# RMSNorm with SiLU on one core: loads and stores in strict turn on the GpSimd queue, 28 tiles ahead

## The chip, the cores and the metric

The kernel runs on one core of a Trainium2 chip. The core has a matrix engine (PE, not used here), VectorE (DVE), ScalarE (ACT), GpSimd (POOL) and SyncE (SP), each with its own instruction stream in program order, and 16 DMA engines that move data between the chip's memory (HBM) and the on-chip memory (SBUF, 128 partitions). Engines wait for each other and for DMAs through semaphores. The metric is device time in microseconds (us) of one execution, smaller being better; the median of several runs is compared.

## What is computed

The input `x` has 8 x 1024 rows of 2048 float32 values. Each row is divided by its root mean square, multiplied by `gamma`, and passed through SiLU:

```python
batch, seq_len, hidden = 8, 1024, 2048
...
rms = np.sqrt(np.mean(x ** 2, axis=-1, keepdims=True) + eps)
out = gamma * x / rms
return (out * (1 / (1 + np.exp(-out)))).astype(np.float32)
```

Input and output are 67.1 MB each, so 134 MB have to pass between HBM and the core.

## The kernel before

The 8192 rows are cut into 64 tiles of 128 rows; a row lies in one partition. In SBUF everything is bfloat16, while HBM holds float32, so each DMA converts: a load reads 8 KB a row and writes 4 KB, a store reads 4 KB and writes 8 KB. All DMAs are issued from GpSimd, on one queue, which the DMA engines work off in order.

`gamma` is first loaded into all partitions (tile `g`, L34). Then one loop over the 64 tiles does, for each of them:

- L42, GpSimd: load rows of `x` into `xt`
- L45, VectorE: `xg = xt * g`
- L48, VectorE: `xt * xt`, written over `xt`, with its row sums in `ss`
- L55, ScalarE: `rms = sqrt(ss / 2048 + eps)`
- L59, VectorE: `rstd = 1 / rms`
- L62, ScalarE: `ot = silu(rstd * xg)`
- L65, GpSimd: store `ot`

Sqrt and Silu use different tables of ScalarE, and where one follows the other the program has an `ACT_TABLE_LOAD`.

Each of `xt`, `xg` and `ot` has a pool of 8 buffers (`bufs=8`), so a load waits until the tile eight earlier has been read. The loop is written tile by tile, but the order that an engine gets is set by a scheduler, which moves instructions of neighbouring tiles past each other: on GpSimd, bursts of loads alternate with runs of stores, and Sqrt and Silu come in small batches. Every DMA on GpSimd counts up one of eight completion semaphores, taken in turn, and the ninth DMA waits for the first.

Of the kernel before, what the change touches and what calls it, by code (L numbers as in the profile page):

```python
# [1 line left out]

# [4 lines left out]


@with_exitstack  # L10
def kernel(
    ctx: ExitStack,
    tc: tile.TileContext,
    x: bass.AP,
    gamma: bass.AP,
    eps: bass.AP,
    out: bass.AP,
):
    nc = tc.nc
    P = nc.NUM_PARTITIONS  # L20
    bf16 = mybir.dt.bfloat16
    f32 = mybir.dt.float32
    x2 = x.flatten_outer_dims()
    o2 = out.flatten_outer_dims()
    n, d = x2.shape
    ntiles = (n + P - 1) // P

    singles = ctx.enter_context(tc.tile_pool(name="singles", bufs=1))
    pool = ctx.enter_context(tc.tile_pool(name="pool", bufs=8))
    small = ctx.enter_context(tc.tile_pool(name="small", bufs=8))  # L30

    g = singles.tile([P, d], bf16)
    gbc = bass.AP(tensor=gamma.tensor, offset=gamma.offset, ap=[[0, P], gamma.ap[0]])
    nc.gpsimd.dma_start(out=g, in_=gbc)  # L34
    eps_t = singles.tile([P, 1], f32)
    nc.vector.memset(eps_t, float(eps))  # L36

    for i in range(ntiles):
        s, e = i * P, min((i + 1) * P, n)
        ts = e - s  # L40
        xt = pool.tile([P, d], bf16)
        nc.gpsimd.dma_start(out=xt[:ts], in_=x2[s:e])  # L42

        xg = pool.tile([P, d], bf16)
        nc.vector.tensor_mul(out=xg[:ts], in0=xt[:ts], in1=g[:ts])  # L45

        ss = small.tile([P, 1], f32)
        nc.vector.tensor_tensor_reduce(  # L48
            out=xt[:ts], in0=xt[:ts], in1=xt[:ts],
            scale=1.0, scalar=0.0,  # L50
            op0=mybir.AluOpType.mult, op1=mybir.AluOpType.add,
            accum_out=ss[:ts],
        )
        rms = small.tile([P, 1], f32)
        nc.scalar.activation(out=rms[:ts], in_=ss[:ts],  # L55
                             func=mybir.ActivationFunctionType.Sqrt,
                             scale=1.0 / d, bias=eps_t[:ts])
        rstd = small.tile([P, 1], f32)
        nc.vector.reciprocal(out=rstd[:ts], in_=rms[:ts])  # L59

        ot = pool.tile([P, d], bf16)
        nc.scalar.activation(out=ot[:ts], in_=xg[:ts],  # L62
                             func=mybir.ActivationFunctionType.Silu,
                             scale=rstd[:ts])
        nc.gpsimd.dma_start(out=o2[s:e], in_=ot[:ts])  # L65


# [1 line left out]
_INS = ['x', 'gamma', 'eps']  # L69
_OUTS = [((8, 1024, 2048), 'float32')]  # L70
#: Inputs that are plain numbers.
_NUMBERS = {'eps': 9.999999747378752e-06}


# [26 lines left out]
```

## Time and profile before

| what | value |
|---|---|
| runs | 337.41, 339.43 and 339.48 us |
| median of the runs | 339.43 us |
| span of the profiled execution, first to last instruction | 336.1 us |
| busy: VectorE, ScalarE, GpSimd | 221.2, 219.1, 69.0 us |
| idle time of GpSimd before stores (L65), waiting for ScalarE | 221.4 us in 64 waits |
| idle time of VectorE before L45, waiting for loads | 95.7 us in 14 waits |
| idle time of ScalarE before L55 | 101.8 us |
| from issue to landing, median: load, store | 15.5 us, 11.5 us |

The profiled execution is listed by its span; the time outside of it is not listed, and the timed runs lie 1.3 to 3.4 us above the span. In a view of instruction groups, a row has the line, engine and operation, output <- input with shapes, the count, then busy time and mean duration (ns), then the idle time of the engine just before these instructions and what ended it. In the 40 slices, each digit is a busy share in tenths, and the row GB/s is what the DMAs wrote. A DMA share can exceed 1, since packets of one engine overlap a little.

### The profile page before, as it was taken

How to read it: one execution, taken by the hardware profiler on the slowest of the kernel's cores; microseconds unless marked ns; L12 is line 12 of the kernel's file. 1: busy time of each engine (PE TensorE's matmuls, PEld its weight loads, DVE VectorE, ACT ScalarE, POOL GpSimd, SP SyncE). 2: the span in 40 equal slices, each digit the busy share in tenths (PEclk: the TensorE clock that was granted, in tenths of full speed). 3: DMA queues.
4: the chain of work that ended last, by engine and by line, in shares of the span. 5: the costliest groups of instructions: out<-in, count | busy, mean ns of one | idle time of the engine just before them, and what ended most of it. 6: DMA issues, size and time to landing. Idle time of an engine off the chain costs nothing.

```text
span 336.1 us, 838 instructions
## 1 busy us (share of the span) xinstructions
DVE 221.2 (66%) x257; ACT 219.1 (65%) x188; POOL 69.0 (21%) x133
## 2 busy tenths in 40 slices
DVE  0999990407999914099999030899991308999900
ACT  1486977522869795238697761386978613869792
POOL 6012111050111110501111105011111050111110
DMA  7999999899999998999999989999999799999997
GB/s 140 212 214 254 335 398 363 332 312 208 214 288 327 402 365 321 324 214 214 291 316 414 366 325 310 214 212 319 307 424 367 286 297 214 213 311 309 420 429 273
DMA packets 18582, 101.24 MB, mean 301 GB/s; under 512 B 2064, under 2 KB 2064, under 8 KB 10384
## 3 DMA queue, kind: packets, MB, share of 16 engines
q0 software_dynamic: 18576, 101.20, 104.1%
q14 instruction: 6, 0.05, 0.0%
HBM read 68.16 MB, written 67.11 MB: 402 GB/s over the span
## 4 chain that ended last, share of the span: by engine, by line
issue 72%; POOL 14%; DMA 11%; POOLq 1%; PEldq 0%
DMA xt<-in_x_dram 11%; POOL out_dram L65 10%; POOL xt L42 4%; POOLq L65 0%; POOL g L34 0%; POOLq L96 0%; POOLq L42 0%; PEldq L96 0%
## 5 line engine op out<-in xcount | busy, mean ns | idle before, releaser
L48 DVE CUSTOM_DVE_ANT_0 xt<-xt 128x2048 bf16<-128x2048 bf16 x64 | 144.8, 2280 | 0.3
L45 DVE TENSOR_TENSOR xg<-xt,g 128x2048 bf16<-128x2048 bf16 x64 | 76.6, 1217 | 95.7 <-DMA xt<-in_x_dram 95.7
L62 ACT ACTIVATE ot<-xg,rstd 128x2048 bf16<-128x2048 bf16 x64 | 124.4, 1993 | 5.8 <-DVE rstd L59 5.5
L55 ACT ACTIVATE rms<-ss,eps_t 128x1 f32<-128x1 f32 x64 | 17.8, 292 | 101.8 <-DVE ss L48 63.7
L65 POOL DMA_DIRECT2D out_dram<-ot x64 | 34.2, 534 | 221.4 <-ACT ot L62 221.4
L42 POOL DMA_DIRECT2D xt<-in_x_dram x64 | 34.1, 554 | 38.8 <-DVE ss L48 22.8
L55 ACT ACT_TABLE_LOAD x30 | 38.5, 1283 | 2.1 <-DVE ss L48 1.0
L62 ACT ACT_TABLE_LOAD x30 | 38.5, 1283 | 0.5
L59 DVE RECIPROCAL rstd<-rms 128x1 f32<-128x1 f32 x64 | 8.6, 153 | 8.4 <-ACT rms L55 8.4
L48 DVE DVE_READ_ACCUMULATOR2_ANT ss<- 128x1 f32 x64 | 5.2, 81 | 0.0
L34 POOL DMA_DIRECT2D g<-in_gamma_dram x1 | 0.7, 667 | 0.8 <-PEq L96 0.8
L36 DVE MEMSET eps_t<- 128x1 f32 x1 | 0.1, 59 | 0.8 <-PEq L82 0.8
L82 POOL MEMSET const-float32-0.0<- 128x1 f32 x1 | 0.1, 99 | 0.2 <-issue 0.2
L82 POOL MEMSET const-bfloat16-1.0<- 128x1 bf16 x1 | 0.1, 102 | 0.0
L82 POOL MEMSET const-float32-1.0<- 128x1 f32 x1 | 0.1, 99 | 0.0
L82 POOL MEMSET const-uint8-127<- 128x1 uint8 x1 | 0.1, 99 | 0.0
## 6 DMA issues: line engine op xcount, KB each, us to landing
out_dram<-ot POOLq DMA_DIRECT2D x64, 1024.0 KB, 11.5
xt<-in_x_dram POOLq DMA_DIRECT2D x64, 512.0 KB, 15.5
g<-in_gamma_dram POOLq DMA_DIRECT2D x1, 512.0 KB, 4.7
```

Of the source, the lines that this page charges most:

```text
L34: nc.gpsimd.dma_start(out=g, in_=gbc)
L36: nc.vector.memset(eps_t, float(eps))
L42: nc.gpsimd.dma_start(out=xt[:ts], in_=x2[s:e])
L45: nc.vector.tensor_mul(out=xg[:ts], in0=xt[:ts], in1=g[:ts])
L48: nc.vector.tensor_tensor_reduce(out=xt[:ts], in0=xt[:ts], in1=xt[:ts], scale=1.0, scalar=0.0, op0=mybir.AluOpType.mult, op1=mybir.AluOpTy ...
L55: nc.scalar.activation(out=rms[:ts], in_=ss[:ts], func=mybir.ActivationFunctionType.Sqrt, scale=1.0 / d, bias=eps_t[:ts])
L59: nc.vector.reciprocal(out=rstd[:ts], in_=rms[:ts])
L62: nc.scalar.activation(out=ot[:ts], in_=xg[:ts], func=mybir.ActivationFunctionType.Silu, scale=rstd[:ts])
L65: nc.gpsimd.dma_start(out=o2[s:e], in_=ot[:ts])
L82: nc = _bacc.Bacc("TRN2", target_bir_lowering=False, num_devices=1)
```

## The change

The whole loop is written anew; four things differ.

- **Order of DMAs.** 28 loads are issued ahead of everything (`LEAD`), and from then on each store is followed by the load of the tile 28 further on, as long as there is one.
- **Buffers.** There is one tile name, `xt`, with 40 buffers. The product with `g` and the Silu are written in place, and the squares go to two scratch tiles that nobody reads (`sq` for ScalarE, `junk` for VectorE).
- **Statistics by fours.** Four tiles share one `ss`, one Sqrt and one reciprocal on 128x4.
- **Squares on two engines.** The sum of squares of even tiles moves to ScalarE (`Square` with an accumulator, L73), that of odd tiles stays on VectorE (L75).

`GRAIN` is 1, so `rows` and `lanes` give whole tiles.

```diff
+    BUFS, LEAD, GRAIN = 40, 28, 1
...
-    pool = ctx.enter_context(tc.tile_pool(name="pool", bufs=8))
+    pool = ctx.enter_context(tc.tile_pool(name="pool", bufs=BUFS))
...
+    def load(i, j):
+        if j == 0:
+            xts[i] = pool.tile([P, d], bf16, name="xt")
+        nc.gpsimd.dma_start(out=lanes(xts[i], j), in_=rows(x2, i, j))
...
+    for i in range(LEAD):
+        for j in range(GRAIN):
+            load(i, j)
...
+        if k % 2 == 0:
+            nc.scalar.activation(out=sq, in_=xts[i], func=ACT.Square, accum_out=acc)
+        else:
+            nc.vector.tensor_tensor_reduce(out=junk, in0=xts[i], in1=xts[i], scale=1.0, scalar=0.0,
+                                           op0=ALU.mult, op1=ALU.add, accum_out=acc)
...
+        nc.scalar.activation(out=rms, in_=ss, func=ACT.Sqrt, scale=1.0 / d, bias=eps_t)
...
+        for i in range(b * GROUP, (b + 1) * GROUP):
+            nc.vector.tensor_mul(out=xts[i], in0=xts[i], in1=g)
+        for i in range(b * GROUP, (b + 1) * GROUP):
+            k = i % GROUP
+            xt = xts.pop(i)
+            nc.scalar.activation(out=xt, in_=xt, func=ACT.Silu, scale=rstd[:, k:k + 1])
+            for j in range(GRAIN):
+                nc.gpsimd.dma_start(out=rows(o2, i, j), in_=lanes(xt, j))
+                if i + LEAD < ntiles:
+                    load(i + LEAD, j)
+
+    for b in range(ntiles // GROUP):
+        for i in range(b * GROUP, (b + 1) * GROUP):
+            stats(i)
+        norm(b)
```

What this does to GpSimd's queue is seen best in its instruction list. `DMASW0` to `DMASW7` are the eight completion semaphores of its DMAs; `DVE` and `Activation` are waits for VectorE and ScalarE. Before, from the eighth load on (the seven before it wait for nothing):

```order
L42 DMA xt<-in_x_dram 128x2048 [waits DMASW0_49]
L42 DMA xt<-in_x_dram 128x2048 [waits DMASW1_49,DVE_49]
L65 DMA out_dram<-ot 128x2048 [waits DMASW2_49,Activation_49]
L42 DMA xt<-in_x_dram 128x2048 [waits DMASW3_49,DVE_49]
L65 DMA out_dram<-ot 128x2048 [waits DMASW4_49,Activation_49]
L65 DMA out_dram<-ot 128x2048 [waits DMASW5_49,Activation_49]
L42 DMA xt<-in_x_dram 128x2048 [waits DMASW6_49,DVE_49]
L42 DMA xt<-in_x_dram 128x2048 [waits DMASW7_49,DVE_49]
L65 DMA out_dram<-ot 128x2048 [waits DMASW0_49,Activation_49]
L65 DMA out_dram<-ot 128x2048 [waits DMASW1_49,Activation_49]
```

After, on the same engine, where the 28 loads end and the pairs begin:

```order
L51 DMA xt<-in_x_dram 128x2048 [waits DMASW2_49]
L51 DMA xt<-in_x_dram 128x2048 [waits DMASW3_49]
L51 DMA xt<-in_x_dram 128x2048 [waits DMASW4_49]
L93 DMA out_dram<-xt 128x2048 [waits DMASW5_49,Activation_49]
L51 DMA xt<-in_x_dram 128x2048 [waits DMASW6_49]
L93 DMA out_dram<-xt 128x2048 [waits DMASW7_49,Activation_49]
L51 DMA xt<-in_x_dram 128x2048 [waits DMASW0_49]
```

The first store now stands behind 28 loads, where it stood behind nine, loads wait for DMAs alone and no longer for VectorE, and loads and stores take strict turns.

On ScalarE, before, a stretch early in the program:

```order
L55 ACT_TABLE_LOAD
L55 ACTIVATE rms<-ss,eps_t 128x1 x3
L62 ACT_TABLE_LOAD
L62 ACTIVATE ot<-xg,rstd 128x2048 x3
L55 ACT_TABLE_LOAD
```

After, its beginning, from the first Square on (`sq` is the scratch tile for squares):

```order
L73 ACTIVATE sq,ss<-xt 128x2048 x3
L83 ACT_TABLE_LOAD
L83 ACTIVATE rms<-ss,eps_t 128x4
L73 ACTIVATE sq,ss<-xt 128x2048
L91 ACT_TABLE_LOAD
L91 ACTIVATE xt<-xt,rstd 128x2048 x4
```

Squares of the following group now stand ahead of a group's Silus, so the first Silu waits for tile 6 as well; a group of four has one Sqrt on 128x4 and two table loads.

More of the change, by code (lines that the diff above doesn't have):

```diff
@@ L7 @@
 from concourse._compat import with_exitstack
+ACT = mybir.ActivationFunctionType
+ALU = mybir.AluOpType
 @with_exitstack
@@ L25, with rows, lanes @@
     n, d = x2.shape
-    ntiles = (n + P - 1) // P
+    ntiles = n // P
+    BUFS, LEAD, GRAIN = 40, 28, 1
     singles = ctx.enter_context(tc.tile_pool(name="singles", bufs=1))
-    pool = ctx.enter_context(tc.tile_pool(name="pool", bufs=8))
+    pool = ctx.enter_context(tc.tile_pool(name="pool", bufs=BUFS))
     small = ctx.enter_context(tc.tile_pool(name="small", bufs=8))
+    def rows(t, i, j):
+        return t[i * P:(i + 1) * P].rearrange("(p g) d -> g p d", g=GRAIN)[j]
+    def lanes(t, j):
+        if GRAIN == 1:
+            return t
+        return t[j:P:GRAIN]
+    xts = {}
+    def load(i, j):
+        if j == 0:
+            xts[i] = pool.tile([P, d], bf16, name="xt")
+        nc.gpsimd.dma_start(out=lanes(xts[i], j), in_=rows(x2, i, j))
     g = singles.tile([P, d], bf16)
@@ L36 @@
     nc.vector.memset(eps_t, float(eps))
[L38 to L65, printed above, removed]
+    sq = singles.tile([P, d], bf16)
@@ new lines, with stats @@
+    for i in range(LEAD):
+        for j in range(GRAIN):
+            load(i, j)
+    GROUP = 4
+    var = {}
+    def stats(i):
+        k = i % GROUP
+        if k == 0:
+            var[i // GROUP] = small.tile([P, GROUP], f32, name="ss")
+        acc = var[i // GROUP][:, k:k + 1]
+        if k % 2 == 0:
[3 more added lines that the diff above has]
+                                           op0=ALU.mult, op1=ALU.add, accum_out=acc)
@@ new lines, with norm @@
+    junk = singles.tile([P, d], bf16, name="junk")
+    def norm(b):
+        ss = var.pop(b)
+        rms = small.tile([P, GROUP], f32, name="rms")
+        nc.scalar.activation(out=rms, in_=ss, func=ACT.Sqrt, scale=1.0 / d, bias=eps_t)
+        rstd = small.tile([P, GROUP], f32, name="rstd")
+        nc.vector.reciprocal(out=rstd, in_=rms)
+        for i in range(b * GROUP, (b + 1) * GROUP):
+            nc.vector.tensor_mul(out=xts[i], in0=xts[i], in1=g)
+        for i in range(b * GROUP, (b + 1) * GROUP):
+            k = i % GROUP
+            xt = xts.pop(i)
[4 more added lines that the diff above has]
+                    load(i + LEAD, j)
```

## The prediction

> **What bounds the kernel now.** I read the page's list of engines first, then its 40 slices.
>
> ```profile
> DVE 221.2 (66%) x257; ACT 219.1 (65%) x188; POOL 69.0 (21%) x133
> ...
> DVE  0999990407999914099999030899991308999900
> ACT  1486977522869795238697761386978613869792
> ...
> DMA  7999999899999998999999989999999799999997
> GB/s 140 212 214 254 335 398 363 332 312 208 214 288 327 402 365 321 324 214 214 291 316 414 366 325 310 214 212 319 307 424 367 286 297 214 213 311 309 420 429 273
> DMA packets 18582, 101.24 MB, mean 301 GB/s; under 512 B 2064, under 2 KB 2064, under 8 KB 10384
> ```
>
> VectorE and ScalarE are each idle for a third of the span; the DMA row is not. Its GB/s counts the bytes written, so a load (1.049 MB of float32 read, 0.524 MB of bfloat16 written) counts half of what a store counts (1.049 MB written). The level near 213 and the level near 427 are therefore the same pace, which pure stretches show best. The next rows are those of a table of stretches: from:to, length, busy time (and instructions) of DVE, ACT and POOL, clock, DMA share, GB/s.
>
> ```profile
> core 0: us, DVE busy (x) ACT busy (x) POOL busy (x), PEclk, DMA share, GB/s
> 8.00:24.00 16.00, 15.06 (x17) 9.79 (x9) 2.13 (x4) 1.00 1.06 213
> ...
> 312.00:328.00 16.00, 7.62 (x12) 13.83 (x13) 2.35 (x5) 1.00 1.12 428
> ...
> 28.50:65.50 37.00, 25.33 (x33) 27.82 (x24) 4.80 (x9) 1.00 1.10 368
> ```
>
> Loads alone run at 213: 0.5243 MB / 213 GB/s = 2.46 us each. Stores alone run at 428: 1.0486 / 428 = 2.45 us each. The third row mixes them: it moves 13.6 MB, which is 4 loads and 11 stores (2.10 + 11.53 MB), 15 DMAs in 37.0 us or 2.47 us each. So a DMA of one tile costs the same 2.46 us in every company. The program has 129 of them (gamma, 64 loads, 64 stores): 34.08 MB / 213 GB/s = 160.0 us and 67.11 MB / 428 GB/s = 156.8 us, together 316.8 us of the 336.1. The kernel is bound by its DMAs, and what a rearrangement can win is the other 19.3 us. I looked for them with the same table:
>
> ```profile
> 0.00:3.00 3.00, 0.06 (x1) 1.28 (x1) 1.94 (x8) 1.00 0.11 20
> 25.00:28.50 3.50, 3.50 (x4) 1.73 (x3) 1.60 (x3) 1.00 1.06 157
> 65.00:68.00 3.00, 0.00 (x0) 3.00 (x2) 0.53 (x1) 1.00 0.30 112
> 74.00:77.00 3.00, 0.00 (x0) 0.00 (x0) 0.53 (x1) 1.00 0.99 146
> 132.00:135.00 3.00, 0.00 (x0) 3.00 (x2) 0.53 (x1) 1.00 0.21 79
> 199.00:202.00 3.00, 0.00 (x0) 2.98 (x3) 0.53 (x1) 1.00 0.40 150
> 207.00:210.00 3.00, 0.00 (x0) 0.00 (x0) 0.53 (x1) 1.00 1.05 178
> 265.00:269.00 4.00, 0.00 (x0) 3.98 (x3) 0.53 (x1) 1.00 0.33 125
> 275.00:278.00 3.00, 0.02 (x1) 0.00 (x0) 0.53 (x1) 1.00 0.95 147
> 330.00:331.00 1.00, 0.00 (x0) 0.00 (x0) 0.28 (x1) 1.00 0.91 344
> 333.00:336.10 3.10, 0.00 (x0) 0.00 (x0) 0.00 (x0) 1.00 0.14 50
> ```
>
> They are of three kinds.
> - Ends. The first 3 us do the work of 20/213 x 3 = 0.3 us, so 2.7 are lost; the last 3.1 do 50/428 x 3.1 = 0.36, so 2.7 are lost.
> - Dry queue. At 65, 132, 199 and 265 the DMA share falls to 0.2 to 0.4: nothing is queued. Lost against 428: 2.2, 2.4, 1.9 and 2.8 us, and 0.2 before the last store, 9.5 in all.
> - Slow but occupied. At 25, 74, 207 and 275 the share stays near 1 and the rate is low. Lost against 213: 0.9, 0.9, 0.5 and 0.9 us, 3.3 in all.
>
> 5.4 + 9.5 + 3.3 = 18.2 of the 19.3; about 1 us is spread thinly. The chain of waits says little here: 72% of it is "issue", GpSimd sitting between DMAs. The waits and the timeline of GpSimd say why the queue runs dry:
>
> ```profile
> POOL out_dram L65 <- ACT ot L62: 221.4, 64, 10.6
> DVE xg L45 <- DMA xt<-in_x_dram: 95.7, 14, 14.0
> ...
> POOL xt L42 <- DMA out_dram<-ot: 6.6, 4, 2.0
> ...
> 6.20 0.53 POOL L42 DMA_DIRECT2D xt<-in_x_dram  x1 [0.56 <-DMA g<-in_gamma_dram]
> ...
> 66.56 0.53 POOL L65 DMA_DIRECT2D out_dram<-ot  x1 [10.58 <-ACT ot L62]
> 68.45 0.53 POOL L65 DMA_DIRECT2D out_dram<-ot  x1 [1.36 <-ACT ot L62]
> 68.97 3.72 POOL L42 DMA_DIRECT2D xt<-in_x_dram  x7
> ```
>
> One in-order queue carries both directions. GpSimd stands 10.6 us at a store whose tile is not computed; the loads for the next tiles stand behind it and go out in a burst only at 68.97. Meanwhile the DMAs empty the queue. VectorE then waits for the burst (95.7 us in all), and the round repeats every 67 us. The line at 6.20 shows a second limit: the ninth DMA waited for the landing of the first (gamma), though it reads nothing of it. Eight completion semaphores serve the queue in turn, so eight DMAs can be outstanding.
>
> **The change part by part.**
>
> *Order on GpSimd.* Gamma and 28 loads go first, then 36 pairs of store and load, then 28 stores. The count of DMAs is unchanged, 129, and no other queue takes any, so 316.8 us of transfers stay. Each DMA still waits for the eighth before it to land. Behind that wait stand all later loads and stores, but seven more DMAs are in flight, 7 x 2.46 = 17 us of cover, against 4.7 us from issue to landing for gamma:
>
> ```profile
> g<-in_gamma_dram POOLq DMA_DIRECT2D x1, 512.0 KB, 4.7
> ```
>
> So this wait costs nothing. GpSimd's issuing, 129 x 0.54 = 70 us spread over the span, is hidden the same way.
>
> *Buffers.* Tile i+28 takes the buffer of tile i-12, whose store stands 24 DMAs earlier in the same queue; the semaphore wait eight back already implies it. No cost.
>
> *Is a store ready when its place comes?* ScalarE's first group runs three Squares, Sqrt, a fourth Square and then the Silus, so store 0 needs tile 6.
>
> ```profile
> 8.57 1.22 DVE L45 TENSOR_TENSOR xg<-xt,g 128x2048 bf16<-128x2048 bf16 x1 [7.70 <-DMA xt<-in_x_dram]
> ...
> L48 DVE CUSTOM_DVE_ANT_0 xt<-xt 128x2048 bf16<-128x2048 bf16 x64 | 144.8, 2280 | 0.3
> L45 DVE TENSOR_TENSOR xg<-xt,g 128x2048 bf16<-128x2048 bf16 x64 | 76.6, 1217 | 95.7 <-DMA xt<-in_x_dram 95.7
> L62 ACT ACTIVATE ot<-xg,rstd 128x2048 bf16<-128x2048 bf16 x64 | 124.4, 1993 | 5.8 <-DVE rstd L59 5.5
> L55 ACT ACTIVATE rms<-ss,eps_t 128x1 f32<-128x1 f32 x64 | 17.8, 292 | 101.8 <-DVE ss L48 63.7
> ...
> L55 ACT ACT_TABLE_LOAD x30 | 38.5, 1283 | 2.1 <-DVE ss L48 1.0
> ```
>
> Tile 0 has landed at 8.6, tile 6 at 8.6 + 6 x 2.46 = 23.3, and after a Square, a table load and a Silu the first output is there at about 29. Its place in the queue is the 30th: 3 + 29 x 2.46 = 74 us. That is 45 us of cover.
>
> *Work per group of four tiles.* A Square is not in the trace; it lies between the Sqrt of 128x1 (0.29 us) and twice the Silu of the same tile (4 us), and I take the Silu's 2.0, the same shape. ScalarE: 2 Squares 4.0, 2 table loads 2.6, one Sqrt 0.3, 4 Silus 8.0 = 14.9 us. VectorE: 2 x 2.28 + 4 x 1.22 and small ones = 9.8 us. The DMAs of four tiles take 8 x 2.46 = 19.7 us, so both stay hidden; with a Square at 4 us ScalarE is at 18.9 and just so. After the prefill ScalarE works off its backlog and then waits for loads, far ahead of the stores. At the end load 63 is the 101st DMA (3 + 101 x 2.46 = 251 us), its group is done some 20 us later, and store 60 moves only at 3 + 125 x 2.46 = 310. So statistics by fours and the in-place tiles cost nothing; if that cover were gone, a store would be late again as at 65 us.
>
> *Dry stretches*: 9.5 us go, all of them.
>
> *Changes of direction.* The mixed stretch held 15 DMAs that by the pure rates take 4 x 2.46 + 11 x 2.45 = 36.8 us, and took 37.0 with 7 changes: 0.03 us each. The new order has 72: 2.1 us, bounds 0 and 2.1.
>
> *Slow but occupied stretches.* Three of four follow a burst of eight loads behind stores, which is no longer there; the first, in the prefill, I keep: 0.9 us, bounds 0 and 3.3.
>
> *Sum.* 316.8 + 5.4 (ends) + 2.1 + 0.9 = 325.2 us of span, against 336.1. What lies outside the span isn't in the page; the timed runs were 337.4 to 339.5 (median 339.4), so 1.3 to 3.4 us above it. With the median's 3.3 I predict 328.5 us, 3.2% faster.
>
> **The rivals.**
>
> *The directions overlap.* If a DMA engine's reading and writing ran side by side, a load (8 KB read, 4 KB written a row) next to a store (4 KB read, 8 KB written) would need 12 KB of time for the pair and not 16: 36 pairs x 4.91 x 1/4 = 44 us less, 284 us. For it: loads write at half the rate at which stores write, so something is idle in each. Against it: the mixed stretch, with whole DMAs alternating as they will now, shows 2.47 us per DMA. The Trainium skill, DMA: Bandwidth & Descriptors, section "Terms", names the two halves of a transfer, reading side and writing side, from which one would hope for this. [...]
>
> *Each turn from store to load stalls.* The rows at 74, 207 and 275 each lie a little behind such a turn and lost 0.5 to 0.9 us, 0.8 on average. Place: the 36 pairs. At that price 36 x 0.8 = 29 us, on 328.5 less about 1 us for those turns counted above: 356 us, slower. Against it: the mixed stretch has three such turns and lost 0.2 us in all. It decides from (339.4 - 328.5) / 36 = 0.3 us a turn, ten times what the mixed stretch shows.
>
> *ScalarE becomes the bound.* If a Square took over 4.4 us (19.7 - 10.9 = 8.8 for two), a group would outlast its transfers. At 6 us: 16 x 22.9 + some 25 at the ends = 391 us. Only an unknown in the accumulating form speaks for it.
>
> **How the numbers follow.** Chances: the queue stays full, 0.84; overlap, 0.03; stalls at turns, 0.10 (half of it at 0.2 to 0.4 us a turn, which is no change); ScalarE the bound, 0.03. The first case alone: low 322.2 + 1.3 = 323.5, less 1 or 2 for the rounding of the rates; high 322.2 + 2.1 + 3.3 + 3.4 = 331. The range goes a little into the stalls, 321.5 to 334. About 1% is what a measurement of this kernel can tell from no change: faster by over 1% 0.87, within 1% 0.05, slower 0.08.
>
> **What would show it.** Right: in the slices the DMA row stays at 9 from the second to the last but one, the GB/s row has three levels (213 for some 70 us, about 318 for 177 us, 428 for 69 us), GpSimd waits mostly for DMA landings eight back and no longer for ScalarE, and ScalarE waits for loads. Wrong: a dip of DMA share inside the span, a middle level well off 318 (higher: overlap; lower: stalls), or stores waiting for Silu late in the program.

## The result, and the profile after

The changed kernel takes 324.67 us (median of four runs, 324.63 to 324.72), the kernel before 339.02 us in the runs beside it (337.41 to 339.48). The ratio is 0.9585, with an interval of 0.9562 to 0.9609: 4.2% faster. The forecast was 328.5 us, in a range of 321.5 to 334. The profiled execution has a span of 322.9 us and a time of 324.65 us.

The page of the changed kernel, its engines and its slices:

```profile
DVE 148.4 (46%) x145; ACT 232.2 (72%) x177; POOL 69.1 (21%) x133
...
DVE  0479897864838474352744543754337410000000
ACT  1449999999999999978949398599799993000000
...
DMA  7999999999999999999999999999999999999997
GB/s 128 214 215 212 213 216 212 212 216 313 308 344 305 318 341 300 326 334 297 334 325 301 339 314 309 343 305 318 343 296 328 400 425 432 426 424 433 425 428 270
DMA packets 18582, 101.24 MB, mean 314 GB/s; under 512 B 2064, under 2 KB 2064, under 8 KB 10384
```

The DMA row is 9 from the second slice to the last but one. The GB/s row has the three levels of the new order: loads alone at 213, pairs of store and load around 320, stores alone at 428. VectorE and ScalarE have nothing left to do in the last six slices, while the stores still queued are written out.

The table of stretches of the changed kernel (columns as before: from:to, length, busy time of DVE, ACT and POOL, clock, DMA share, GB/s), at the start, where two of the old holes were, in the phase of the pairs, and at the end:

```profile
0.00:3.00 3.00, 0.06 (x1) 1.28 (x1) 1.94 (x8) 1.00 0.26 22
3.00:6.00 3.00, 0.00 (x0) 0.00 (x0) 2.64 (x5) 1.00 0.96 184
...
65.00:68.00 3.00, 0.81 (x2) 2.96 (x5) 0.53 (x1) 1.00 1.05 210
74.00:77.00 3.00, 2.42 (x3) 3.00 (x3) 0.56 (x2) 1.00 1.12 386
...
80.00:240.00 160.00, 82.65 (x81) 138.10 (x105) 34.71 (x65) 1.00 1.09 321
...
320.00:322.90 2.90, 0.00 (x0) 0.00 (x0) 0.00 (x0) 1.00 0.04 11
```

A pair writes 1.049 + 0.524 = 1.573 MB. At 321 GB/s it takes 4.90 us, 2.45 us a DMA, the price of the pure stretches: turning the direction with every DMA costs nothing that can be measured.

The waits of the changed kernel, the longest totals first (engine, line, what it waited for: total us, times, longest):

```profile
POOL out_dram L93 <- DMA out_dram<-xt: 97.9, 47, 2.2
POOL xt L51 <- DMA xt<-in_x_dram: 96.4, 56, 2.0
DVE junk L75 <- DMA xt<-in_x_dram: 86.5, 22, 10.5
...
POOL out_dram L93 <- ACT xt L91: 17.8, 7, 4.5
```

GpSimd now waits for landings eight DMAs back, about 2 us at a time and with seven DMAs still queued. The last row still puts 17.8 us down to Silu, where it was 221.4 us before, but these too are waits for landings: a wait for several semaphores is put down to the one that moved last, and the tiles had long been done. The view of tile `xt` has the first and the last start of the Silus and of the stores (after the durations in ns):

```profile
L91 ACT ACTIVATE xt<-xt,rstd x64: 1984/1986/2003, 27.1 to 267.4; 128x2048 bf16<-128x2048 bf16 x64
L93 POOL DMA_DIRECT2D out_dram<-xt x64: 533/538/542, 58.6 to 302.1; - x64
```

Taken pair by pair in the trace, every Silu ended 29 to 74 us before GpSimd issued its store; for the store with the wait of 4.5 us it was 48 us. No store was late.

### The profile page after: what moved, and what is told of

The parts are those of the page before. It is cut to its first block, busy times and chain, and to the rows that moved or that the text cites. A ratio compares the mean times of both kernels' runs of the same rounds, so it can differ in the third digit from the quotient of the medians.

```text
span 322.9 us, 639 instructions
## 1 busy us (share of the span) xinstructions
DVE 148.4 (46%) x145; ACT 232.2 (72%) x177; POOL 69.1 (21%) x133
## 4 chain that ended last, share of the span: by engine, by line
DMA 88%; issue 3%; ACT 2%; POOL 1%; POOLq 0%; DVE 0%; PEldq 0%
DMA xt<-in_x_dram 70%; DMA out_dram<-xt 18%; ACT xt L91 2%; POOL xt L51 0%; POOL g L55 0%; POOLq L131 0%; DVE rstd L85 0%; DVE ss L75 0%; POOLq L93 0%; DVE junk L75 0%; PEldq L131 0%
## 5 line engine op out<-in xcount | busy, mean ns | idle before, releaser
L91 ACT ACTIVATE xt<-xt,rstd 128x2048 bf16<-128x2048 bf16 x64 | 122.9, 1990 | 21.3 <-DVE rstd L85 21.1
L75 DVE CUSTOM_DVE_ANT_0 junk<-xt 128x2048 bf16<-128x2048 bf16 x32 | 73.3, 2290 | 86.5 <-DMA xt<-in_x_dram 86.5
L87 DVE TENSOR_TENSOR xt<-xt,g 128x2048 bf16<-128x2048 bf16 x64 | 75.5, 1217 | 12.2 <-ACT sq L73 9.0
L73 ACT ACTIVATE sq<-xt 128x2048 bf16<-128x2048 bf16 x32 | 60.8, 1901 | 14.5 <-DMA xt<-in_x_dram 14.1
L93 POOL DMA_DIRECT2D out_dram<-xt x64 | 34.3, 536 | 135.0 <-DMA out_dram<-xt 97.9
L85 DVE RECIPROCAL rstd<-rms 128x4 f32<-128x4 f32 x16 | 2.8, 175 | 12.7 <-ACT rms L83 12.7
L73 ACT ACTIVATION_READ_ACCUMULATOR sq<-xt 128x1 f32 x32 | 6.0, 186 | 0.0
L83 ACT ACTIVATE rms<-ss,eps_t 128x4 f32<-128x4 f32 x16 | 4.8, 297 | 0.2
L75 DVE DVE_READ_ACCUMULATOR2_ANT ss<- 128x1 f32 x32 | 2.6, 83 | 0.0
```

The lines of the kernel that those rows point to most:

```text
L73: nc.scalar.activation(out=sq, in_=xts[i], func=ACT.Square, accum_out=acc)
L75: nc.vector.tensor_tensor_reduce(out=junk, in0=xts[i], in1=xts[i], scale=1.0, scalar=0.0, op0=ALU.mult, op1=ALU.add, accum_out=acc)
L83: nc.scalar.activation(out=rms, in_=ss, func=ACT.Sqrt, scale=1.0 / d, bias=eps_t)
L85: nc.vector.reciprocal(out=rstd, in_=rms)
L87: nc.vector.tensor_mul(out=xts[i], in0=xts[i], in1=g)
L91: nc.scalar.activation(out=xt, in_=xt, func=ACT.Silu, scale=rstd[:, k:k + 1])
```

## The experiments

Each was timed beside the kernel before, which had medians of 338.9, 338.8 and 338.2 us in the three groups (runs 1 to 4, 5 to 8, 9 to 12).

**1. The kernel before once more.** No edit.

> The kernel before, unchanged, to see what comes back at the same place. Theory: the four dry stretches (DMA share 0.2 to 0.4 near 65, 132, 199 and 265 us) are set by the order of the program and come back there, 9 to 10 us in all; the slow but occupied stretches are an effect of the moment and move or differ in size; the time lies 1.7 to 1.8 us above the span, as after the change. Rival: the slow stretches are made by the program too (by bursts of eight loads) and come back at 74, 207 and 275 us with 0.5 to 0.9 us each.

Measured: 339.06 us (337.5 to 340.04); the profiled execution took 338.78 us with a span of 337.0. The same table of it:

```profile
25.00:28.50 3.50, 3.50 (x4) 1.92 (x4) 1.60 (x3) 1.00 1.02 169
65.00:68.00 3.00, 0.00 (x0) 3.00 (x2) 0.53 (x1) 1.00 0.28 107
74.00:77.00 3.00, 0.08 (x1) 0.00 (x0) 0.53 (x1) 1.00 1.05 179
132.00:135.00 3.00, 0.00 (x0) 3.00 (x2) 0.53 (x1) 1.00 0.07 25
141.00:144.00 3.00, 0.00 (x0) 0.00 (x0) 0.53 (x1) 1.00 1.02 158
199.00:202.00 3.00, 0.00 (x0) 3.00 (x2) 0.53 (x1) 1.00 0.20 74
208.00:211.00 3.00, 0.00 (x0) 0.00 (x0) 0.53 (x1) 1.00 1.01 156
266.00:270.00 4.00, 0.00 (x0) 3.98 (x3) 0.53 (x1) 1.00 0.42 158
275.00:278.00 3.00, 0.00 (x0) 0.00 (x0) 0.53 (x1) 1.00 1.02 154
```

The dry stretches are back in place: 2.2, 2.8, 2.5 and 2.5 us against 428 GB/s, 10.0 us. The four slow but occupied stretches are back in place too, 0.5 to 0.8 us each, and there is a fifth at 141 us, 0.8 us, where the first profile had 206 GB/s and lost 0.1 us. So the rival was right on the places, which belong to this program; how much is lost at each differs between executions. The time outside the span is 1.8 us here and 1.75 us after the change.

**2. More buffers, same order.**

```diff
-    pool = ctx.enter_context(tc.tile_pool(name="pool", bufs=8))
+    pool = ctx.enter_context(tc.tile_pool(name="pool", bufs=14))
```

> The kernel before with 14 buffers for each of its three tiles; GpSimd's order stays exactly the same. Theory (the order makes the queue run dry, since a store that is not ready holds the loads behind it): the dry stretches stay, time 333 to 339 us. Rival (buffers were short): 325 to 328 us.

Measured: 339.01 us, ratio 1.0005 (0.9979 to 1.0031). GpSimd's instructions come in the same order as before, and the dry stretches stay: 175 GB/s from 66 to 69 us, 38 from 132 to 135, 55 from 267 to 270. Buffers alone do nothing as long as stores hold the loads behind them in the queue.

**3. The order alone.** The arithmetic of before, tile by tile, three tiles, all squares on VectorE; 24 loads ahead, then store and load in turn. The loads get 32 buffers, and the product and the output five each, where before had eight.

```diff
-    pool = ctx.enter_context(tc.tile_pool(name="pool", bufs=8))
+    xpool = ctx.enter_context(tc.tile_pool(name="xpool", bufs=32))
+    pool = ctx.enter_context(tc.tile_pool(name="pool", bufs=5))
+    LEAD = 24
...
+    for i in range(LEAD):
+        load(i)
...
+        if i + LEAD < ntiles:
+            load(i + LEAD)
```

> The arithmetic of before, tile by tile, with three tiles and all squares on VectorE, but 24 loads ahead and then stores and loads in turn. Theory (the order alone wins): 324.5 to 327 us, as long as ScalarE holds 4.9 us a tile; its 94 table loads, 64 Sqrts and 64 Silus come to 263 us, 4.1 us a tile. Rival (the grouping by fours is needed, since Sqrt, reciprocal and Silu of one tile wait for each other): ScalarE at 5.2 us a tile or more, stores late, 335 to 345 us.

Measured: 334.18 us, ratio 0.9866 (0.9843 to 0.9889): a third of the gain, outside the range of the theory and just short of the rival's. The queue was full for 288 us, and then ran dry four times, among the last stores:

```profile
288.00:292.00 4.00, 3.88 (x4) 4.00 (x3) 0.53 (x1) 1.00 0.43 162
301.00:304.00 3.00, 2.97 (x4) 3.00 (x3) 0.69 (x2) 1.00 0.40 150
310.00:314.00 4.00, 3.96 (x5) 3.99 (x3) 0.53 (x1) 1.00 0.27 100
320.00:323.00 3.00, 0.00 (x0) 3.00 (x2) 0.53 (x1) 1.00 0.35 131
```

Against 428 GB/s that is 2.5 + 1.9 + 3.1 + 2.1 = 9.6 us. ScalarE is busy throughout in these rows: once only stores are left, the queue takes a tile every 2.45 us, and ScalarE's lead was used up. Where the lead was lost stands in the waits of this kernel:

```profile
ACT ot L69 <- DMA out_dram<-ot: 29.1, 4, 23.0
```

The first store could move only behind 24 loads, the five output buffers were full long before, and ScalarE stood 23 us. In the phase of the pairs it could not win them back: with one tile at a time it has two table loads of 1.28 us, a Sqrt of 0.29 and a Silu of 2.00, together 4.85 us, and a pair takes 4.91.

**4. All squares on VectorE, in the changed kernel.**

```diff
-        if k % 2 == 0:
+        if False:
```

> The changed kernel with all squares on VectorE. VectorE then has 64 x 2.29 + 64 x 1.22 = 225 us and ScalarE 172 us. Theory (both lie beside the DMAs): the same 324.5 to 325.0 us. Rival (VectorE's 3.6 us a tile with its waits delays stores): over 326 us.

Measured: 324.83 us (324.75 to 324.91), with VectorE busy 218.6 us and ScalarE 168.7. Splitting the squares over two engines is worth 0.2 us at most.

**5 and 6. Shorter leads, in the changed kernel.**

```diff
-    BUFS, LEAD, GRAIN = 40, 28, 1
+    BUFS, LEAD, GRAIN = 20, 7, 1
```

> The changed kernel with LEAD 7 and 20 buffers; the scheduler puts 12 loads first and soon settles on store i, load i+7. A group's statistics then need a load that was issued only a few DMAs before the group's first store. Theory (a full queue is all that counts): the queue runs dry once a group, some 2 to 8 us in each of about 14 groups, 350 to 430 us. Rival (seven tiles ahead are enough): 325 us.

```diff
-    BUFS, LEAD, GRAIN = 40, 28, 1
+    BUFS, LEAD, GRAIN = 20, 12, 1
```

> The changed kernel with LEAD 12 and 20 buffers. Between the load of a group's last tile and the group's first store stand 16 DMAs, 39 us, and a group's work is some 15 us. Theory (a full queue is all that counts): 324.5 to 325.2 us, as with 28. Rival (the depth of 28 tiles is needed): 328 us or more.

Measured: 327.81 us with 7 tiles, 325.61 us with 12. The forecast for 7 was far off, and 12 lies 0.4 us above its range. With 7 tiles the scheduler put a group's squares behind the Silus of the group before, so no group waited for loads of the next. GpSimd still stood up to 12 us before a group's first store (222.0 us of waits for Silu in all), but eight queued DMAs are 8 x 2.46 = 19.7 us of work and bridged that. Before the last four stores no loads are left to queue; there GpSimd stood 14.1 us, and one dry stretch is left:

```profile
310.00:315.00 5.00, 0.00 (x0) 4.99 (x4) 1.06 (x2) 1.00 0.50 188
```

That is 5 x (1 - 188/428) = 2.8 us of the 3.1 us between this kernel and the changed one. With 12 tiles no dry stretch is left; 0.9 us remain, of which a slow but occupied stretch before the first store (33 to 36 us, 186 GB/s) is 0.4.

**7. Stores on another queue.** Silu writes float32 tiles, and SyncE stores them without converting; 16 loads ahead, 24 buffers, eight output tiles.

```diff
-            nc.scalar.activation(out=xt, in_=xt, func=ACT.Silu, scale=rstd[:, k:k + 1])
+            yt = ypool.tile([P, d], f32, name="yt")
+            nc.scalar.activation(out=yt, in_=xt, func=ACT.Silu, scale=rstd[:, k:k + 1])
             for j in range(GRAIN):
-                nc.gpsimd.dma_start(out=rows(o2, i, j), in_=lanes(xt, j))
+                nc.sync.dma_start(out=rows(o2, i, j), in_=lanes(yt, j))
```

> The changed kernel with Silu writing float32 tiles, which SyncE stores on its own queue without converting; loads stay on GpSimd, 16 ahead, 24 buffers. Loads and stores now alternate packet by packet inside a DMA engine. Theory (a DMA engine works on one packet at a time and 8 KB a row cost the same in any company): 129 x 2.455 = 316.7 us stay, 323 to 327 us. Rival (reading and writing overlap once they alternate finely): below 310 us.

Measured: 328.79 us, 1.8 us above the range of the theory. In the phase with both directions:

```profile
80.00:240.00 160.00, 75.93 (x75) 120.88 (x94) 17.08 (x33) 1.00 1.04 316
```

316 GB/s against 321 in the changed kernel, which over 160 us is about 2.5 of the 4.2 us by which the span is longer. Two queues that offer both directions at the same time move no more than one queue that turns with every tile, so reading and writing do not overlap to any gain here.

**8 and 12. Gamma as one row.** One row of 8 KB is loaded, and TensorE spreads it over the partitions; in run 12 its DMA goes third, behind two loads.

```diff
-    nc.gpsimd.dma_start(out=g, in_=gbc)
+    nc.gpsimd.dma_start(out=grow, in_=g1)
+    ones = singles.tile([1, P], bf16, name="ones")
+    nc.vector.memset(ones, 1.0)
...
+    for c in range(0, d, 512):
+        nc.tensor.matmul(gp[:, c:c + 512], lhsT=ones, rhs=grow[:, c:c + 512], start=True, stop=True)
+    nc.vector.tensor_copy(out=g, in_=gp)
```

> The changed kernel, with gamma loaded as one row of 8 KB and spread to the partitions by TensorE (four matmuls with a column of ones) and one copy, in place of a DMA of 128 rows. Theory (each whole DMA costs 2.46 us of the end): 322.1 to 322.5 us. Rival (the first DMA is hidden in the start-up): 324.7 us.

> The kernel with gamma as one row, its small DMA issued behind the first two loads and not ahead of them. Theory (the small DMA ahead of all others delayed the first load by 0.4 us): 322.4 to 322.7 us. Rival: no difference to gamma first, 322.98 us.

Measured: 322.98 us (322.89 to 323.06) with gamma first, 322.43 us (322.37 to 322.51) with gamma third, ratio to before 0.9541 (0.9515 to 0.9568). Run 8 lies between its theory and its rival, run 12 in the range of its theory. A whole DMA less is worth 2.2 us of its 2.46, once its small successor is out of the way of the first load: the first 6 us move 77 GB/s with gamma first and 96 with gamma third, which at 213 GB/s is 0.5 us of loads. This version is faster than both kernels.

**9. Order and in-place buffers without the grouping.** One tile at a time, all squares on VectorE, 28 ahead, 40 buffers.

```diff
-    GROUP = 4
+    GROUP = 1
...
-        if k % 2 == 0:
+        if False:
```

> The changed kernel with statistics of one tile at a time and all squares on VectorE: order and 40 in-place buffers stay, the grouping goes. The scheduler makes 44 table loads of it, so ScalarE has 199 us of work and VectorE 225. Theory (in the order-only kernel ScalarE lost 23 us early because its five output buffers were full until the first store could move, and that debt came out as dry stretches in the last 28 stores; buffers, not the grouping, were what it lacked): 324.5 to 325.5 us. Rival (the grouping by fours is needed): 330 us or more.

Measured: 324.65 us (324.42 to 324.70), the time of the changed kernel. Neither the grouping in the program nor the split of the squares is needed. Batches as such were not taken away: 44 table loads for 64 tiles mean that the scheduler still put about three tiles between two switches of table. Nearly single tiles, with 88 table loads, are in run 11.

**10. Bursts in place of turns.** Each group loads its own four tiles when it begins, 24 buffers; the order that results has 12 loads, then 12 stores.

```diff
-    BUFS, LEAD, GRAIN = 40, 28, 1
+    BUFS, LEAD, GRAIN = 24, 0, 1
...
         for i in range(b * GROUP, (b + 1) * GROUP):
+            load(i, 0)
+        for i in range(b * GROUP, (b + 1) * GROUP):
             stats(i)
...
-                if i + LEAD < ntiles:
-                    load(i + LEAD, j)
```

> The changed kernel without the lead: each group of four loads its tiles when it begins, 24 in-place buffers; the scheduler makes bursts of 12 loads and 12 stores of it. Theory (only an empty queue costs; a burst of 12 loads is 29 us of cover, and the four stores that need the last loads have eight stores, 20 us, ahead of them against some 15 us of work): 325 to 329 us, without dry stretches but for the end, with slow but occupied stretches of 0.5 to 0.9 us after each turn from stores to loads. Rival (strict turns are needed): 332 us or more, dry stretches of 2 us and more in each round.

Measured: 337.29 us, ratio 0.9976 (0.9958 to 0.9995). The time is the rival's, but not its reason. The one large hole is at the end:

```profile
313.00:323.00 10.00, 5.77 (x6) 7.11 (x7) 0.54 (x1) 1.00 0.07 22
```

10 x (1 - 22/428) = 9.5 us of the 12.6 us in span over the changed kernel: the last four tiles were loaded last, and nothing was queued while they were computed. The other 3.1 us are the difference and were not placed one by one; in the rounds before, no 3 us lose more than about 0.5 us to a gap in the queue (352 GB/s from 114 to 117 us is the worst). I had expected the loads to turn slow behind the stores; they did not.

**11. The order alone, with ten output buffers.**

```diff
-    xpool = ctx.enter_context(tc.tile_pool(name="xpool", bufs=32))
-    pool = ctx.enter_context(tc.tile_pool(name="pool", bufs=5))
-    LEAD = 24
+    xpool = ctx.enter_context(tc.tile_pool(name="xpool", bufs=24))
+    pool = ctx.enter_context(tc.tile_pool(name="pool", bufs=10))
+    LEAD = 20
```

> The order-only kernel with ten buffers for each of the product and the output (20 loads ahead, 24 buffers for the loads). Theory (output buffers held ScalarE back): ScalarE's early wait for stores shrinks from 23 us to some 5 or less, the dry stretches at the end shrink from 9.7 us to 0 to 4, 325 to 329 us. Rival (ScalarE's pace with single tiles is at fault): 333 to 335 us as before.

Measured: 325.16 us, ratio 0.9620 (0.9598 to 0.9643). ScalarE's longest wait for a store fell from 23.0 to 5.4 us, and no dry stretch is left:

```profile
ACT ot L69 <- DMA out_dram<-ot: 19.1, 9, 5.4
```

The lead is four loads shorter here than in run 3, so the first store also moves some 10 us sooner, and this pair of runs alone does not separate the two. Run 9 does: with the long lead of 28 and 40 in-place buffers nothing is lost. This is what the in-place tiles are good for: each of the 40 buffers is an output buffer as well, and ScalarE can run ahead while the first 28 loads block the stores.

## Why the prediction was right, and where its sum was off

- **What bounds the kernel.** Right. 129 DMAs at 2.46 us were 316.8 us of the forecast; the changed kernel is that plus its ends, 322.9 - 316.8 = 6.1 us. Taking one DMA away (run 12) took 2.2 us away; taking ScalarE's squares away (run 4) took nothing.
- **Dry stretches.** Right: all 9.5 us went. Run 1 shows that they belong to the order of before, run 2 that more buffers do not fill them. What the step left out is that the order needs somewhere to put outputs. It called the in-place tiles free, which they are, but with few output buffers the same holes come back at the end (run 3, 9.6 us) and go again with more (runs 9 and 11).
- **Stores ready when their place comes.** Right: the first output was ready at 29.1 us, as forecast, and every later one 29 us or more before its store was issued. A Square was taken at 2.0 us; it measured 1.90 us, with 0.19 us more to read its accumulator.
- **Changes of direction.** The term was 2.1 us and measured 0: in the phase of the pairs a DMA costs 2.45 us. The 0.2 us that stood behind the 0.03 us a change came from a single stretch of 37 us with 7 changes; over 160 us with some 65 changes nothing is left of it.
- **Slow but occupied stretches.** The term was 0.9 us; the changed kernel has none. All 3.3 us of them went, and with the 9.5 us above that is 12.8 of the 13.2 us by which the span fell. The reading that they follow bursts of loads behind stores fell with run 10, which has such bursts and no such loss behind them. Two patterns are left. In the kernel before, all but the first come 7 to 10 us after a dry stretch, and run 10 had none of those ahead of its bursts. And the kernels with at most 24 loads ahead of the first store (before, runs 3, 5, 6, 7, 10 and 11) each had one just before that store, where the packets of loads took 0.45 us and more in the traces, against 0.32 elsewhere; those with 28 (the changed kernel, runs 4, 8, 9 and 12) lost nothing there. Their cause is open.
- **Ends.** 5.4 us forecast, 6.1 left over above the transfers. The rows that the forecast went by give nearly what it said, 2.7 us in the first 3 us and 2.8 in the last 2.9. Another 0.4 us is lost from 3 to 6 us (184 GB/s where loads reach 213), which the forecast left out; the last 0.2 us are not placed.
- **Time outside the span.** This was the second largest miss: 3.3 us, by setting the median of the runs against a span from another execution. It measured 1.75 us after the change and 1.8 us in run 1, where time and span belong to the same execution.
- Together: 328.5 - 2.1 - 0.9 + 0.7 - 1.55 = 324.65 us. Three of the four misses made the forecast too slow, so the gain came out at 4.2% and not 3.2%; it was not luck that brought the time into the range, since the two large terms, 316.8 us of transfers and 9.5 us of dry stretches, hold by themselves.
- **Rivals.** Overlap of directions: refuted, by 321 GB/s in the pairs and by run 7. Stalls at turns from store to load: refuted, 36 of them cost nothing. ScalarE as the bound: it did not come near, at 232 us of work in 322.9.

## What to carry to other kernels

Where DMAs bound a kernel and both directions share one in-order queue, count the DMAs by their price alone, and look for the places where the queue runs empty; apart from DMAs that can be left out (run 12), only those can be won. A load that stands behind a store that is not ready costs time as soon as that wait outlasts what is still queued: waits of some 12 us behind eight queued DMAs cost nothing in run 5, and a wait of 10.6 us emptied the shorter queue of the kernel before. So put enough loads ahead, and give the computing engine enough output buffers to keep working until the first store has its turn, or the debt is paid among the last stores. The last tile's load should be followed by enough stores to cover that tile's computation.

## What the runs showed of the hardware

- A converting DMA does not cost by the bytes that it writes, nor by those that it reads: a load that reads 1.05 MB and writes 0.52 takes 2.46 us, and a store that reads 0.52 MB and writes 1.05 takes 2.45 us. Both have 1.05 MB of float32 on the side of HBM, and both have 128 x 2048 elements; no run here tells which of these sets the time. A plain float32 store beside a converting load (run 7) was not cheaper: 316 GB/s where 321 were reached with converting stores.
- Strict turns of direction have no price: 321 GB/s over 160 us, in which a pair of pure transfers would give 1.573 MB / 4.91 us = 320.
- A table load of ScalarE adds its own 1.28 us and little more: in the changed kernel's timeline the Sqrt ends at 260.43, the load runs from 260.44, and the Silu starts at 261.74.

```profile
260.13 0.30 ACT L83 ACTIVATE rms<-ss,eps_t 128x4 f32<-128x4 f32 x1
260.44 1.28 ACT L91 ACT_TABLE_LOAD   x1
261.74 7.68 ACT L91 ACTIVATE xt<-xt,rstd 128x2048 bf16<-128x2048 bf16 x4
```
